# An mLSTM and dilated-attention trunk: whole operands for the 128-column products of layer B, and another order of issue in layer A and at the turn

## The chip, the cores and the metric

The kernel runs on one core of a Trainium2 chip. A core has TensorE for matmuls (PE in the profile; PEld is its weight load), VectorE (DVE), ScalarE (ACT), GpSimd (POOL) and SyncE (SP), which here issues all DMAs. They work in parallel, each in its own order of instructions, and wait for each other through semaphores. The metric is the time of one execution on the device, in microseconds; the median of several runs counts.

## The reference

A sequence of 1024 tokens with 1024 channels goes through two layers. Layer A is an mLSTM: an input projection to three times 2048 channels, a causal convolution, block-diagonal queries, keys and values, a recurrence over chunks with 4 heads, a gate, an output projection and a LayerNorm. Layer B is attention with 8 heads of 128 channels in three groups g = 0, 1, 2, of dilation 1, 4 and 16, which are merged by their softmax denominators.

```python
def mlstm_layer(x, w_in, conv_w, conv_b, wq, wk, wv, w_if, b_if, gn_g, skip, w_out):
    xm, z, o_pre = jnp.split(x @ w_in, 3, axis=-1)
    xc = jax.nn.silu(causal_dwconv(xm, conv_w, conv_b))
    q = headwise(xc, wq)
    k = headwise(xc, wk)
    v = headwise(xm, wv)
...
    h = ((h - mu) * lax.rsqrt(var + LN_EPS)).reshape(bsz, s, INNER_A) * gn_g
    y = (h.astype(x.dtype) + skip * xc) * jax.nn.silu(z)
    return y @ w_out
...
        x = layer_norm(ALPHA * x + y, ln_g[layer], ln_b[layer])
```

In layer B a block of 128 queries sees its own block of 128 keys and, where there is one, the block ahead of it with the same residue of the dilation.

## The kernel before

All products are of 32-bit numbers. `mm3` (lines 97 to 99) makes one of three matmuls in the faster fp32r format: of two operands, each split into a high and a low part, it adds high by high, high by low and low by high. `split` makes the parts: ScalarE copies the high one (line 92), VectorE subtracts it to get the low one (line 93). Where neither operand has been split, a plain F32 matmul of the whole operands is used, as for all of g = 2 (lines 1200 and 1266; each stands in a loop that passes it 8 times in each of the 8 heads, 64 times in all). The larger projections go by Strassen's scheme, in `strassen_steps` and `strassen_wide`, seven block products with sums on VectorE.

The tile framework orders each engine's instructions with a scheduler of its own; the program gives the work, in an order of code, and fixed slots of SBUF (s0 to s52) and banks of PSUM (b0 to b7). `issue_after` binds what it encloses to stand behind a given instruction on its engine. All DMAs are issued by SP, in its one order.

By the time in the profile: up to 379 us the input projection of layer A, its streams of two 128-channel blocks (`stream`) and the z gates. Beside the first streams, `setup` makes on GpSimd the block-diagonal matrices for the values, the gates' weights, and the matrices "A" by which queries and keys meet in the scores (`through`, `spread`, four splits on GpSimd, stores into DRAM). From 391 to 535 us comes the o projection (`strassen_wide`, two pairs of blocks), with the gates' tables between. Attention of layer A (`layer_a_attend`, up to 810 us) goes over 4 heads and 2 halves of the tokens; `prep_q` makes queries, `scores` the first blocks' scores, `finish` joins skip path and gate; the convolved channels xc are loaded before it begins. The out projection (`layer_a_out`, 810 to 987 us) goes over two halves of the tokens; in the second half the first half's rows are transposed to be operands of layer B (`x1`), and `scale_row` applies the LayerNorm's gain and shift for the residual. The last rows are transposed by line 987 at the turn (987 to 1045 us).

Layer B goes over two quads of heads, in each over g = 0, 1, 2, in each over 4 heads: `queries_keys`, `scores`, `attend`. In `attend`, `transposed` turns the weights of up to four 128x128 blocks and splits them, and `av` multiplies them by the values.

Of the kernel before, what the change touches and what calls it, by code (L numbers as in the profile page):

```python
# [11 lines left out]
F32R = mybir.dt.float32r  # L12
# [48 lines left out]
class Kernel:  # L61
# [226 lines left out]
    def strassen_wide(self, raw, x, banks, dest, done, eng):  # L288
# [49 lines left out]
        product(d, b11, x["s1"], True)  # L338
        result(1, 1, u3, d)
        product(c, b21, x["22"], False)  # L340
        result(1, 0, u2, c)
        product(d, b22, x["s4"], False)
        result(0, 1, u2, d)

# [20 lines left out]
    def build(self):  # L365
        nc, tc = self.nc, self.tc
        with ExitStack() as top:
# [35 lines left out]
            self.layer_b()  # L403


    def setup(self):
# [5 lines left out]
        w3 = self.slot(50, (P, 4, NC_A, 4))  # L412
# [3 lines left out]
        wkr = self.slot(52, (P, NC_A, 4, 4))  # L416
        nc.sync.dma_start(wkr, a["wkr"])

        def spread(dst, src, n):
            G.tensor_tensor(dst.rearrange("p c (n j) -> p c n j", j=4),  # L420
                            src.unsqueeze(2).to_broadcast([P, n, 32, 4]),
                            self.mask.unsqueeze(1).unsqueeze(3).to_broadcast([P, n, 32, 4]), op=ALU.mult)

        def through(dst, w, rep, m):

            G.tensor_tensor(rep, rep, w.unsqueeze(3).to_broadcast([P, NC_A, 4, m]), op=ALU.mult)
            G.tensor_tensor(rep[:, :, 0:2], rep[:, :, 0:2], rep[:, :, 2:4], op=ALU.add)
            G.tensor_tensor(dst, rep[:, :, 0], rep[:, :, 1], op=ALU.add)

        self.wv = []  # L430
        for i, c0 in enumerate((0, 7, 14)):
# [4 lines left out]
            spread(t[:, :, 0:P], wvT[:, c0:c0 + n], n)  # L436
        g3 = self.t(cp, [P, 3, NC_A, 8], tag="k2")
        gates = []
        for i, w in enumerate((wqT, wkT, wvT)):
# [3 lines left out]
            through(g, w, rep, 8)  # L443
# [6 lines left out]
        at = w3[:, 3]  # L450
        through(at, wqT, wkr, 4)
        for i in range(2):
            bd = self.slot(51, (P, 8, P))
            spread(bd, at[:, 8 * i:8 * i + 8], 8)
# [7 lines left out]
    def layer_a_project(self):  # L462
# [1112 lines left out]
```

## Time and profile before

| | |
|---|---|
| median of 3 runs | 2061.74 us (2061.1 to 2061.84) |
| the profiled execution, its own time | 2060.43 us |
| its span | 2058.5 us |
| TensorE busy | 1992.0 us, 97% |
| VectorE busy | 1468.4 us, 71% |
| ScalarE busy | 1001.4 us, 49% |
| GpSimd busy | 155.1 us, 8% |
| mean granted clock of TensorE | 0.991 |

The span runs from the first to the last instruction of the profiled execution; its own time is 1.9 us longer. The shares of busy time are means over the span. The granted clock is in parts of full speed.

### The profile page before, as it was taken

What the parts mean: (1) busy time and instruction counts of PE and PEld (TensorE: products, weight loads), DVE (VectorE), ACT (ScalarE), POOL (GpSimd) and SP (SyncE); (2) the same over time, 40 slices, a digit from 0 to 9 for tenths busy, and PEclk for the clock granted to TensorE, in tenths of its full rate; (3) what the DMA queues carried; (4) which work ended last, traced back from release to release, by engine and by line L of the source; (5) the groups of instructions that cost most, each with busy time, mean ns of one, the idle gap of its engine ahead of it and who ended that gap; (6) DMA issues with size and microseconds to landing.
All of it is one profiled execution on the core that took longest, in us unless ns stands there. A gap on an engine that the chain in (4) does not pass through costs nothing.

```text
span 2058.5 us, 28088 instructions
## 1 busy us (share of the span) xinstructions
PE 1992.0 (97%) x10336; PEld 1684.8 (82%) x10336; DVE 1468.4 (71%) x2843; ACT 1001.4 (49%) x1920; POOL 155.1 (8%) x127
## 2 busy tenths in 40 slices
PE   8989999999999999989899999999999999999897
PEld 6868888788788888868788998888888898888786
DVE  8777788674566776475777757756878757757888
ACT  5455555535545543333534636645625635656531
POOL 0130000001145442000000000000000000000000
PEclk9999999999999999999999999999999999999999
DMA  4454565455754443424123131222542232123753
GB/s 166 145 193 168 190 209 180 145 176 201 246 189 171 176 176 135 155 96 160 57 87 123 43 133 52 75 99 103 186 159 101 73 114 72 52 97 110 262 202 123
DMA packets 112945, 288.12 MB, mean 140 GB/s; under 512 B 13028, under 2 KB 34980, under 8 KB 112808
## 3 DMA queue, kind: packets, MB, share of 16 engines
q1 hardware_dynamic: 112808, 286.34, 39.3%
q8 instruction: 81, 1.33, 0.3%
q14 instruction: 56, 0.46, 0.1%
HBM read 200.00 MB, written 86.30 MB: 139 GB/s over the span
## 4 chain that ended last, share of the span: by engine, by line
PE 80%; DVE 9%; DMA 6%; issue 2%; ACT 2%; SPq 0%; DVEq 0%; ACTq 0%
PE b L98 25%; PE b L99 25%; PE b L97 25%; DMA s<-df 3%; DVE s L93 3%; PE b L578 1%; PE b L1223 1%; DVE s L141 1%; PE b L584 1%; PE b L852 1%; DVE s L1340 1%; ACT s L92 1%; DVE s L543 1%; DMA s<-in_w_xm 0%; DMA s<-dc 0%
## 5 line engine op out<-in xcount | busy, mean ns | idle before, releaser
L98 PE MATMUL b<-s,s 128*128 128x512 f32 (+3 forms) x3032 | 1102.1, 366 | 12.1 <-DVE s L93 12.0
L97 PE MATMUL b<-s,s 128*128 128x512 f32 (+2 forms) x3032 | 1082.6, 367 | 26.5 <-ACT s L92 18.3
L99 PE MATMUL b<-s,s 128*128 128x512 f32 (+3 forms) x3032 | 1086.9, 365 | 4.0 <-DVE s L93 3.9
L92 ACT CAST s<-s 128x512 fp32r<-128x512 f32 (+4 forms) x674 | 434.5, 659 | 550.4 <-PE b L99 316.1
L93 DVE TENSOR_TENSOR s<-s,s 128x512 fp32r<-128x512 f32 (+2 forms) x670 | 510.8, 772 | 243.2 <-ACT s L92 240.9
L97 PEld LDWEIGHTS b<-s,s 128*128 128x128 f32 x3032 | 573.6, 190 | 123.2 <-ACT s L92 23.0
L98 PEld LDWEIGHTS b<-s,s 128*128 128x128 f32 x3032 | 576.0, 190 | 100.1 <-DVE s L93 14.3
L99 PEld LDWEIGHTS b<-s,s 128*128 128x128 f32 x3032 | 574.1, 190 | 96.4 <-DVE s L93 7.6
L230 DVE TENSOR_TENSOR s<-s,b 128x512 f32<-128x512 f32 x168 | 114.2, 682 | 56.0 <-PE b L99 52.8
L1210 ACT ACTIVATE s<-s,nmax 128x128 f32<-128x128 f32 (+1 forms) x192 | 84.5, 441 | 38.8 <-DVE nmax L1208 38.0
L224 DVE TENSOR_TENSOR s<-s,b 128x512 f32<-128x512 f32 x112 | 75.8, 680 | 25.2 <-PE b L99 24.8
L93 DVE TENSOR_TENSOR s<-b,s 128x512 fp32r<-128x512 f32 (+1 forms) x96 | 59.0, 630 | 45.7 <-ACT s L92 45.3
L543 DVE SCALAR_TENSOR_TENSOR s<-s,c_convw,s 128x512 f32<-128x512 f32 (+3 forms) x96 | 73.4, 772 | 2.3 <-ACT s L540 1.8
L745 POOL TENSOR_TENSOR s<-s 128x512 fp32r<-128x512 f32 x32 | 43.0, 1357 | 405.9 <-ACT s L744 396.0
L1206 DVE CUSTOM_DVE_ANT_0 s<-b,k 128x128 f32<-128x128 f32 (+1 forms) x192 | 57.8, 346 | 17.5 <-PE b L99 17.4
L786 ACT ACTIVATE s<-s,k 128x128 f32<-128x128 f32 x144 | 47.2, 392 | 41.8 <-DVE s L93 21.5
L243 DVE TENSOR_TENSOR s<-s,s 128x512 f32<-128x512 f32 (+1 forms) x52 | 38.2, 735 | 38.5 <-DMA s<-in_w_xm 15.3
L92 ACT CAST s<-b 128x512 fp32r<-128x512 f32 (+1 forms) x96 | 50.2, 545 | 30.6 <-PE b L99 18.4
L1159 ACT ACTIVATE s<-s 128x512 fp32r<-128x512 f32 x48 | 42.0, 881 | 11.3 <-DVE s L230 11.1
L856 POOL TENSOR_TENSOR s<-s,s 128x512 f32<-128x512 f32 x32 | 42.3, 1337 | 65.5 <-DVE s L855 50.9
L1160 DVE SCALAR_TENSOR_TENSOR s<-s,s 128x512 fp32r<-128x512 f32 x48 | 42.2, 885 | 5.7 <-ACT s L1159 5.3
L1223 PE MATMUL b<-c_ident,s 128*128 128x128 f32 x280 | 44.8, 276 | 0.3 <-ACT s L1210 0.3
(177 smaller groups left out, 1420.6 us busy)
## 6 DMA issues: line engine op xcount, KB each, us to landing
s<-in_w_qk SPq DMA_DIRECT2D x48, 512.0 KB
s<-in_w_out SPq DMA_DIRECT2D x40, 512.0 KB
dp<-s SPq DMA_DIRECT2D x32, 512.0 KB
s<-dp SPq DMA_DIRECT2D x32, 512.0 KB
s<-in_w_z SPq DMA_DIRECT2D x24, 512.0 KB
s<-in_w_v SPq DMA_DIRECT2D x24, 512.0 KB
dg<-s SPq DMA_DIRECT2D x24, 512.0 KB
s<-dg SPq DMA_DIRECT2D x24, 512.0 KB
```

What stands on the lines that cost most here:

```text
L92: self.nc.scalar.copy(h, src)
L93: (l_eng or self.nc.vector).tensor_tensor(l, src, f(h), op=ALU.subtract)
L97: mm(ps, lh, rh, start=start, stop=False, skip_group_check=skip)
L98: mm(ps, lh, rl, start=False, stop=False, skip_group_check=skip)
L99: mm(ps, ll, rh, start=False, stop=stop, skip_group_check=skip)
L224: V.tensor_tensor(o, p, q, op=add)
L230: V.tensor_tensor(o, p[lane][rows], q[lane][rows], op=add)
L543: V.scalar_tensor_tensor(u[i][:, lo:o + 512], xm[i][:, lo - s:o + 512 - s], convw[:, c, 3 - s:4 - s], u[i][:, lo:o + 512], op0=ALU.mult, o ...
L786: A.activation(E[:, i * P:i * P + P], src[:, i * P:i * P + P], AF.Exp, bias=self.bias[:, hd, ig, j:j + 1])
L1206: V.tensor_tensor_reduce(out=dst, in0=sc, in1=bias, op0=ALU.add, op1=ALU.max, scale=1.0, scalar=-3e38, accum_out=mx[:, b:b + 1])
L1210: A.activation(res[b][0], res[b][0], AF.Exp, bias=nm[:, b:b + 1], accum_out=stat[:, 1, g, b:b + 1])
L1223: T.transpose(pt[:, i * P:i * P + P], src, self.ident)
```

## The change

1. Whole operands. In layer B the products of 128 columns are made of whole F32 operands by one matmul instead of three: in each head the four scores of g = 1 that have no block ahead, three value products of g = 0 and four of g = 1. ScalarE writes the whole queries and keys of the first half of g = 1 into slot 52 (`whole`), and copies the turned weights of these products (`pw`); the parts of a split that nobody reads any more are left out.
2. The matrices "A" are no longer made in `setup` but in `setup_scores`, at the first step of the second pair of the o projection.
3. `strassen_wide`, the gates' tables and the attention become generators, so that parts of the latter two can stand between steps of the o projection: attention's preparation behind step 5 of the second pair, first queries and scores behind step 6. xc is loaded head by head. Banks 0 to 3 and 4 to 7 change places in layer A's projection, and two of the z gates stand behind other streams.
4. In the second half of the out projection the splits of `x1` and the residual's scaling are dealt out over steps c = 5 to 10, each bound to stand behind that step's last split.
5. The last transposes of layer A stand behind layer B's first product step.
6. Slots: the residual's scaling keeps slot 52, which the whole operands now use too; some other slots change places.

The core of the diff:

```diff
     def split(self, h, l, src, l_eng=None):
         self.nc.scalar.copy(h, src)
-        (l_eng or self.nc.vector).tensor_tensor(l, src, f(h), op=ALU.subtract)
+        self.last_split = (l_eng or self.nc.vector).tensor_tensor(l, src, f(h), op=ALU.subtract)
...
         product(a, b11, x["11"], True)
+        yield
         for o, p in zip(u2, a):
             A.copy(o, p)
         product(a, b21, x["12"], False)
+        yield
         done(0, 0, a)
...
+            self.attend = self.layer_a_attend()
             self.layer_a_project()
-            self.layer_a_attend()
+            for _ in self.attend:
+                pass
             self.layer_a_out()
...
+    def setup_scores(self):
+        nc, a = self.nc, self.a
+        t = self.slot(40)
+        w, wkr, at = [t[:, lo:hi] for lo, hi in ((0, 64), (64, 320), (320, 384))]
+        w, at = [v.rearrange("p (c i) -> p c i", i=4) for v in (w, at)]
+        wkr = wkr.rearrange("p (c i m) -> p c i m", i=4, m=4)
+        nc.sync.dma_start(w, a["wqT"])
+        nc.sync.dma_start(wkr, a["wkr"])
+        self.through(at, w, wkr, 4)
         for i in range(2):
-            bd = self.slot(51, (P, 8, P))
-            spread(bd, at[:, 8 * i:8 * i + 8], 8)
+            bd = self.slot(41 + i, (P, 8, P))
+            self.spread(bd, at[:, 8 * i:8 * i + 8], 8)
             for j in range(2):
                 cs = slice(512 * j, 512 * j + 512)
-                h, l = self.pair(52)
-                self.split(h, l, bd.rearrange("p c m -> p (c m)")[:, cs], G)
-                nc.sync.dma_start(self.dram["A", i][:, 0, cs], f(h))
-                nc.sync.dma_start(self.dram["A", i][:, 1, cs], f(l))
+                hl = self.slot(43 + j, (P, 2, 512), F32R)
+                self.split(hl[:, 0], hl[:, 1], bd.rearrange("p c m -> p (c m)")[:, cs], nc.gpsimd)
+                nc.sync.dma_start(self.dram["A", i][:, :, cs], f(hl))
...
             mid = last_values(c2)
-            if c2 in (1, 3, 5, 7):
+            if c2 in (0, 2, 5, 7):
                 if c2 == 7:
                     self.w_raw = Ring(32, 33)
-                for _ in gates(z, ones, szs, mid):
+                for _ in gates(z, ones, szs, mid if c2 else None):
                     pass
-                mid, z = None, z + 1
+                mid, z = None if c2 else mid, z + 1
...
-            self.strassen_wide([raw[n] for n in range(4)], x, ((0, 1, 2, 3), (4, 5, 6, 7)), place, sigmoid, V)
-            if pair == 0:
-                columns()
-        self.xc = []
-        for c in range(NC_A):
-            self.xc.append(self.slot((20, 21, 22, 23, 24, 25, 26, 27, 16, 17, 18, 19, 28, 29, 30, 31)[c]))
-            nc.sync.dma_start(self.xc[c], self.dram["xc", c])
+            steps = self.strassen_wide([raw[n] for n in range(4)], x, ((4, 5, 6, 7), (0, 1, 2, 3)), place, sigmoid, V)
+            beside = ({3: lambda: next(tables), 7: lambda: next(tables, None)},
+                      {1: self.setup_scores, 5: lambda: next(self.attend), 6: lambda: next(self.attend)})[pair]
+            for n, _ in enumerate(steps, 1):
+                beside.get(n, lambda: None)()
...
-        q_slots = (44, 45, 46, 47)
+        q_slots = (44, 45, 46, 52)
...
         prep_x(0, 0)
-        prep_q(0, 0)
         prep_v(0, 0)
         st = begin(0, 0)
-        ahead = [scores(0, 0, 0, st), scores(0, 0, 1, st)]
+        yield
+        prep_q(0, 0)
+        ahead = [scores(0, 0, 0, st)]
+        yield
+        ahead.append(scores(0, 0, 1, st))
+        self.xc = []
...
+                if j == 1 and half == 0:
+                    for c in range(HC * hd, HC * hd + HC):
+                        t = self.slot((20, 21, 22, 23, 24, 25, 26, 27, 16, 17, 18, 19, 28, 29, 30, 31)[c])
+                        nc.sync.dma_start(t, self.dram["xc", c])
+                        self.xc.append(t)
...
-                        self.x1["11"], self.x1["12"]
                         gain, shift = self.ln_params(0, 12, 39)
-                        for tb in range(4):
-                            self.scale_row(rows[tb], gain, shift)
-                            nc.sync.dma_start(self.dram["x1", tb], rows[tb])
+                if half and c in (5, 6):
+                    with self.tc.issue_after(self.last_split.ins):
+                        self.x1[("11", "12")[c - 5]]
+                if half and 7 <= c < 11:
+                    with self.tc.issue_after(self.last_split.ins):
+                        self.scale_row(rows[c - 7], gain, shift)
+                    nc.sync.dma_start(self.dram["x1", c - 7], rows[c - 7])
...
-        transposes((4, 5, 6), Ring(0, 1, 2, 3))
-        self.a_last = lambda: transposes((7,), Ring(4, 5))
+        self.a_last = lambda: [transposes((4, 5, 6), Ring(2, 3, 4, 5)), transposes((7,), Ring(6, 7))]
...
-                next(steps), next(steps)
+                next(steps)
+                self.a_last()
+                next(steps)
                 self.w_raw, u_slots, self.u_slots = Ring(50, 51), self.u_slots, Ring(13)
-                ahead = gates(0, (52, 48), ((7,), (1,), (2,), (3,)))
+                ahead = gates(0, (47, 48), ((7,), (1,), (2,), (3,)))
                 next(ahead), next(ahead)
                 self.u_slots = u_slots
-                self.a_last()
...
+            whole = self.slot(52, (P, 2, 4, P)) if g == 1 else None
...
+                if g == 1 and half == 0:
+                    A.activation(whole[:, i], sv, AF.Copy, scale=scale)
+                    if i == 0:
+                        return
...
+                    elif g == 1 and b % 2 == 0:
+                        T.matmul(ps[:, o:o + w], whole[:, 0, b // 2], whole[:, 1, b // 2], start=True, stop=True,
+                                 skip_group_check=True)
...
-                    self.split(ph[:, 0:n], pl[:, 0:n], pt[:, 0:n])
+                    m = n - P * n_whole
+                    self.split(ph[:, 0:m], pl[:, 0:m], pt[:, 0:m])
+                    if n_whole:
+                        pw = self.t(cp, [P, 2, P], tag="pw", bufs=2)
+                        A.copy(pw[:, 0:n_whole].rearrange("p j n -> p (j n)"), pt[:, m:n])
+                        return ph, pl, pw
...
+            def av_whole(bank, o, kb, p2, j, start):
+                T.matmul(po[bank][:, o:o + P], v[kb][2], p2[2][:, j], start=start, stop=True,
+                         skip_group_check=True)
...
                     if b2 == 1:
-                        av(0, 384, P, 3, p2, 256, False)
-                        av(1, 0, P, 3, p2, 384, True)
+                        av_whole(0, 384, 3, p2, 0, False)
+                        av_whole(1, 0, 3, p2, 1, True)
                     elif b2 == 3:
-                        av(1, 384, P, 7, p2, 256, False)
+                        av_whole(1, 384, 7, p2, 0, False)
                     else:
-                        av(bank, (b % 4) * P + P, 256, b + 1, p2, 256, False)
+                        av(bank, (b % 4) * P + P, b + 1, p2, 256, False)
...
-                    p2 = transposed(q0, q1[:, 0:P], q1[:, P:256])
+                    p2 = transposed(q0, q1[:, 0:P], q1[:, P:256], n_whole=1)
                     at = 256 * (r % 2)
-                    av(r // 2, at, 256, 2 * r, p2, 0, r % 2 == 0)
-                    av(r // 2, at + P, P, 2 * r + 1, p2, 256, False)
+                    av(r // 2, at, 2 * r, p2, 0, r % 2 == 0)
+                    av_whole(r // 2, at + P, 2 * r + 1, p2, 0, False)
```

On ScalarE at the start of attention: before, with L854 the skip scaling of xc, L636 the o gate's activation, and the casts from banks (b) the high parts of the first queries.

```order
L854 ACTIVATE s_739_4314<-s_739_4314,c_skip_3147 128x512 x2
L854 ACTIVATE s_740_4316<-s_740_4316,c_skip_3147 128x512 x2
L636 ACTIVATE s_725_4278<-s_725_4278 128x512 x2
L636 ACTIVATE s_726_4279<-s_726_4279 128x512 x2
L92 CAST s_749_4336<-b_748_4332 128x512
L92 CAST s_751_4343<-b_750_4339 128x512
L854 ACTIVATE s_741_4318<-s_741_4318,c_skip_3147 128x512 x2
L92 CAST s_753_4350<-b_752_4346 128x512
L854 ACTIVATE s_742_4320<-s_742_4320,c_skip_3147 128x512 x2
L92 CAST s_755_4357<-b_754_4353 128x512
```

After, where L870 is the skip scaling and L653 the o gate:

```order
L92 CAST s_733_4249<-b_732_4245 128x512
L92 CAST s_735_4256<-b_734_4252 128x512
L870 ACTIVATE s_1144_6468<-s_1144_6468,c_skip_3118 128x512 x2
L870 ACTIVATE s_1145_6470<-s_1145_6470,c_skip_3118 128x512 x2
L653 ACTIVATE s_747_4356<-s_747_4356 128x512 x2
L92 CAST s_737_4263<-b_736_4259 128x512
L92 CAST s_739_4270<-b_738_4266 128x512
L653 ACTIVATE s_748_4357<-s_748_4357 128x512 x2
```

The first two casts now stand ahead of the skip scaling, the next two behind two pairs of it.

On VectorE in the second half of the out projection: before, with L909 and L910 the residual's gain and shift, L991 an eviction of transposes, and L93 the subtractions, of `x1` from s_1356 to s_1365, of w_out and of the running rows otherwise.

```order
L93 TENSOR_TENSOR s_1373_7853<-s_1359_7783,s_1372_7852 128x1024
L909 TENSOR_TENSOR s_1316_7512<-s_1316_7512,s_1378_7864 128x1024
L909 TENSOR_TENSOR s_1318_7537<-s_1318_7537,s_1378_7864 128x1024
L909 TENSOR_TENSOR s_1320_7562<-s_1320_7562,s_1378_7864 128x1024
L991 TENSOR_SCALAR s_1365_7809<-b_1367_7816,c_lnT_7008 128x512
L909 TENSOR_TENSOR s_1327_7611<-s_1327_7611,s_1378_7864 128x1024
L93 TENSOR_TENSOR s_1375_7857<-s_1362_7796,s_1374_7856 128x1024
L910 TENSOR_TENSOR s_1316_7512<-s_1316_7512,s_1379_7865 128x1024
L910 TENSOR_TENSOR s_1318_7537<-s_1318_7537,s_1379_7865 128x1024
L910 TENSOR_TENSOR s_1320_7562<-s_1320_7562,s_1379_7865 128x1024
L93 TENSOR_TENSOR s_1377_7861<-s_1365_7809,s_1376_7860 128x1024
L910 TENSOR_TENSOR s_1327_7611<-s_1327_7611,s_1379_7865 128x1024
```

After, where L934 and L935 are gain and shift:

```order
L93 TENSOR_TENSOR s_1381_7916<-s_1356_7767,s_1380_7915 128x1024
L93 TENSOR_TENSOR s_1383_7920<-s_1359_7780,s_1382_7919 128x1024
L93 TENSOR_TENSOR s_1384_7923<-s_888_5094,s_1384_7923 128x512
L93 TENSOR_TENSOR s_1392_7964<-s_889_5096,s_1392_7964 128x512
L93 TENSOR_TENSOR s_1387_7929<-s_1385_7926,s_1386_7928 128x1024
L93 TENSOR_TENSOR s_1389_7957<-s_1362_7793,s_1388_7956 128x1024
L93 TENSOR_TENSOR s_1391_7961<-s_1365_7806,s_1390_7960 128x1024
L93 TENSOR_TENSOR s_1396_8000<-s_1015_5779,s_1396_8000 128x512
L93 TENSOR_TENSOR s_1395_7970<-s_1393_7967,s_1394_7969 128x1024
L934 TENSOR_TENSOR s_1316_7509<-s_1316_7509,s_1370_7845 128x1024
L93 TENSOR_TENSOR s_1399_8006<-s_1397_8003,s_1398_8005 128x1024
L934 TENSOR_TENSOR s_1318_7534<-s_1318_7534,s_1370_7845 128x1024
```

Subtractions of the running products now stand between those of `x1`, and the scaling comes behind them, an operation at a time.

On TensorE at the turn: before, the last products of the out projection and then the transposes (L987), of which 26 stand in a row.

```order
L98 MATMUL b_1369_7823<-s_1427_8177,s_1424_8171 128x512
L99 MATMUL b_1369_7823<-s_1426_8176,s_1424_8171 128x512
L987 MATMUL b_1447_8353<-c_ident_246,s_1428_8180 128x128
L987 MATMUL b_1447_8353<-c_ident_246,s_1430_8211 128x128
L987 MATMUL b_1448_8358<-c_ident_246,s_1428_8180 128x128
L987 MATMUL b_1448_8358<-c_ident_246,s_1430_8211 128x128
```

After, with the transposes as L1012 and layer B's first products in banks b_1456 and b_1457, 48 of which stand ahead of the first transpose:

```order
L99 MATMUL b_1457_8366<-s_1488_8499,s_1389_7957 128x256
L97 MATMUL b_1457_8366<-s_1488_8499,s_1388_7956 128x256
L1012 MATMUL b_1475_8452<-c_ident_246,s_1428_8177 128x128
L1012 MATMUL b_1475_8452<-c_ident_246,s_1430_8208 128x128
L1012 MATMUL b_1475_8452<-c_ident_246,s_1432_8239 128x128
L98 MATMUL b_1457_8366<-s_1488_8499,s_1388_7956 128x256
L99 MATMUL b_1457_8366<-s_1488_8499,s_1389_7957 128x256
L1012 MATMUL b_1476_8457<-c_ident_246,s_1428_8177 128x128
L1012 MATMUL b_1476_8457<-c_ident_246,s_1430_8208 128x128
L1012 MATMUL b_1476_8457<-c_ident_246,s_1432_8239 128x128
```

The transposes have moved behind and in between products of layer B.

## Rows read from the trace of the kernel before

**Rows 1.** The page: the span, and section 1

```profile
span 2058.5 us, 28088 instructions
...
PE 1992.0 (97%) x10336; PEld 1684.8 (82%) x10336; DVE 1468.4 (71%) x2843; ACT 1001.4 (49%) x1920; POOL 155.1 (8%) x127
```

**Rows 2.** TensorE's waits over the span: us, times, longest

```profile
PE b L97 <- ACT s L92: 18.3, 11, 6.4
PE b L98 <- DVE s L93: 12.0, 5, 4.8
```

**Rows 3.** Stretches: length, busy time (instructions) of PE, PEld, DVE, ACT, POOL, clock, DMA share, GB/s

```profile
120.00:140.00 20.00, 14.68 (x63) 10.98 (x62) 18.27 (x28) 10.57 (x20) 7.60 (x4) 0.91 0.67 249
480.00:520.00 40.00, 40.00 (x178) 33.12 (x177) 20.03 (x30) 28.34 (x52) 1.50 (x1) 1.00 0.69 245
535.00:550.00 15.00, 10.78 (x46) 7.71 (x45) 5.29 (x8) 9.26 (x16) 0.00 (x0) 1.00 0.86 303
900.00:930.00 30.00, 22.24 (x99) 16.66 (x98) 21.16 (x22) 13.37 (x18) 0.00 (x0) 0.89 0.45 163
985.00:1000.00 15.00, 10.88 (x67) 9.15 (x66) 8.91 (x31) 8.74 (x12) 0.00 (x0) 0.89 0.35 141
1010.00:1040.00 30.00, 26.52 (x182) 24.45 (x181) 26.85 (x33) 15.72 (x22) 0.00 (x0) 0.94 0.08 28
1079.00:1088.00 9.00, 7.25 (x24) 5.22 (x23) 6.95 (x11) 2.89 (x5) 0.00 (x0) 0.81 0.41 152
1550.00:1800.00 250.00, 250.00 (x1478) 221.06 (x1478) 181.76 (x388) 129.50 (x282) 0.00 (x0) 1.00 0.24 83
```

**Rows 4.** Line 1266, and timelines of TensorE: start, us, instruction

```profile
L1266 PE MATMUL b<-s,s x128: 270/275/275, 1417.3 to 1968.0; 128*128 128x128 f32 x128
...
1417.30 1.05 PE L1266 MATMUL b<-s,s 128*128 128x128 f32 x8
...
552.04 0.27 PE L97 MATMUL b<-s,s 128*128 128x128 f32 x1
552.15 0.27 PE L98 MATMUL b<-s,s 128*128 128x128 f32 x1
```

**Rows 5.** Groups of two shapes: busy us, mean ns, idle before

```profile
L1159 ACT ACTIVATE s<-s 128x512 fp32r<-128x512 f32 x48 | 42.0, 881 | 11.3 <-DVE s L230 11.1
...
L93 POOL TENSOR_TENSOR s<-s,s 128x512 fp32r<-128x512 f32 x4 | 6.7, 1663 | 16.0 <-ACT s L92 16.0
```

**Rows 6.** Timeline beside the first streams

```profile
118.96 0.68 DVE L93 TENSOR_TENSOR s<-s,s 128x512 fp32r<-128x512 f32 x1
...
124.66 2.24 POOL L420 TENSOR_TENSOR s<-s,em 128x1024 f32<-128x1024 f32 x1
125.06 2.39 DVE L93 TENSOR_TENSOR s<-s,s 128x512 fp32r<-128x512 f32 x1
...
129.47 0.41 PE L584 MATMUL b<-s,k 128*16 128x512 f32 x1 [4.45 <-ACT s L92]
```

**Rows 7.** Timeline at the start of attention

```profile
535.77 2.63 ACT L854 ACTIVATE s<-s,c_skip 128x512 f32<-128x512 f32 x4 [4.78 <-DMA s<-dc]
...
541.00 0.68 PE L97 MATMUL b<-s,s 128*128 128x512 f32 x2 [2.34 <-ACT s L92]
```

**Rows 8.** Timelines of VectorE and TensorE in the out projection

```profile
907.66 3.49 DVE L909 TENSOR_TENSOR s<-s,s 128x1024 f32<-128x1024 f32 x3
...
921.60 0.80 PE L98 MATMUL b<-s,s 128*128 128x512 f32 x1 [4.81 <-DVE s L93]
```

**Rows 9.** Timeline at the turn to layer B

```profile
990.65 4.38 PE L987 MATMUL b<-c_ident,s 128*128 128x128 f32 x21 [3.38 <-ACT s L972]
```

**Rows 10.** Timeline at the first heads of layer B

```profile
1074.39 0.32 SPq L1053 DMA_DIRECT2D s<-dx  x1
...
1078.03 1.22 DVE L909 TENSOR_TENSOR s<-s,s 128x1024 f32<-128x1024 f32 x1 [1.73 <-DMA s<-dx]
...
1080.48 0.19 PEld L97 LDWEIGHTS b<-s,s 128*128 128x128 f32 x1 [1.13 <-ACT s L92]
```

More of the change, by code (lines that the diff above doesn't have):

```diff
@@ L411, in setup @@
         self.mask = self.const("mask32", [P, 32], tag="em")
-        w3 = self.slot(50, (P, 4, NC_A, 4))
+        w3 = self.slot(50, (P, 3, NC_A, 4))
         for i, n in enumerate("qkv"):
@@ L415, in setup @@
         wqT, wkT, wvT = w3[:, 0], w3[:, 1], w3[:, 2]
[L416 to L428, printed above, removed]
         self.wv = []
@@ L435, in setup @@
                 self.wv.append(t[:, c])
-            spread(t[:, :, 0:P], wvT[:, c0:c0 + n], n)
+            self.spread(t[:, :, 0:P], wvT[:, c0:c0 + n], n)
         g3 = self.t(cp, [P, 3, NC_A, 8], tag="k2")
@@ L442, in setup @@
             g = g3[:, i]
-            through(g, w, rep, 8)
+            self.through(g, w, rep, 8)
             gates.append(g)
@@ L503, in layer_a_project @@
         halves = lambda h: slice(512 * h, 512 * h + 512)
-        ones = ((0,), (1,), (2,), (3,))
+        ones = ((4,), (5,), (6,), (7,))
         def gates(c2, banks, szs, mid=None, raw=None):
@@ L520, in layer_a_project @@
         quarters = lambda p: [t[:, 512 * i:512 * i + 512] for t in wz[p] for i in range(2)]
-        for _ in zip_longest(*[gates(p, ((p,), (p,), (4 + p,), (p,)), szs, raw=quarters(p)) for p in range(4)]):
+        for _ in zip_longest(*[gates(p, ((4 + p,), (4 + p,), (p,), (4 + p,)), szs, raw=quarters(p)) for p in range(4)]):
             pass
@@ L609, in layer_a_project @@
             A.copy(gs[:, 512 * half:512 * half + 512], psg[half][0:16, :])
-        columns = self.gate_tables(gs, gx, pv)
+        tables = self.gate_tables(gs, gx, pv)
+        next(tables)
         self.w_hl, self.u_slots = Ring(36, 37, 49, 47), Ring(8, 9, 10, 11)
@@ L705, in gate_tables @@
                           self.dram["G"].unsqueeze(0).to_broadcast([P, HA, 64]))
-        def columns():
-            cols = self.bank(pv)[:, 0:64].rearrange("p (s b h) -> p s b h", s=2, h=4)
-            for s, r in enumerate((ar, em)):
-                for j in range(8):
-                    T.transpose(cols[:, s, j], r[:, j * P:j * P + P], self.ident[0:4, 0:4])
-            self.em = self.t(cp, [P, 8, HA], tag="em")
-            V.tensor_copy(self.em, cols[:, 1])
-            for h in range(HA):
-                V.tensor_tensor(self.bias[:, h], cols[:, 0, :, h].unsqueeze(1).to_broadcast([P, 8, 8]), self.bias[:, h],
-                                op=ALU.add)
-        return columns
+        yield
+        cols = self.bank(pv)[:, 0:64].rearrange("p (s b h) -> p s b h", s=2, h=4)
+        for s, r in enumerate((ar, em)):
+            for j in range(8):
+                T.transpose(cols[:, s, j], r[:, j * P:j * P + P], self.ident[0:4, 0:4])
+        self.em = self.t(cp, [P, 8, HA], tag="em")
+        V.tensor_copy(self.em, cols[:, 1])
+        for h in range(HA):
+            V.tensor_tensor(self.bias[:, h], cols[:, 0, :, h].unsqueeze(1).to_broadcast([P, 8, 8]), self.bias[:, h],
+                            op=ALU.add)
     def layer_a_attend(self):
@@ L1143, in head_values @@
             at = lambda b: (b // 4, b % 4) if g == 0 else (b % 2, b // 2)
-            return [(h[:, at(b)[0], at(b)[1]], l[:, at(b)[0], at(b)[1]]) for b in range(8)]
+            whole = lambda half, t: v[half][i].rearrange("p (t n) -> p t n", t=4)[:, t, cs]
+            return [(h[:, at(b)[0], at(b)[1]], l[:, at(b)[0], at(b)[1]], whole(*at(b))) for b in range(8)]
         def queries_keys(h, g):
@@ L1163, in queries_keys @@
             self.strassen(self.quarters(a["w_qk"][g, h]), x, ones, None, done, V)
-            return [(None, th[i], tl[i]) for i in range(2)]
+            return [(whole, th[i], tl[i]) for i in range(2)]
         def table(h, g):
@@ L1175, in scores @@
         def scores(h, g, qk, stat):
-            (_, qh, ql), (_, kh, kl) = qk
+            (whole, qh, ql), (_, kh, kl) = qk
             tb = table(h, g)
```

41 lines of the change are left out of this document (27 added, 14 removed).

## The prediction

> **What bounds the kernel now.** I read the page first. TensorE is busy for 97% of the span [rows 1]: the most that better order can return is the 66 us in which it is idle, and what it loses while its granted clock is low. VectorE at 71% and ScalarE at 49% are not the bound over the whole, but each can be over a few microseconds. The waits of TensorE, sorted by releaser, come second: the largest are for the two halves of a split, the copy on ScalarE (18.3 us in 11 waits) and the subtraction on VectorE (12.0 us in 5) [rows 2]. Eleven and five: a few places lose, not a steady rate. So the third view is a table of stretches, where each loss can be priced. The reader is to see in it that the long stretch of attention in layer B is full (250.00 of 250 us, clock 1.00), and that five short stretches in layer A, in the turn to layer B and at its first heads are not [rows 3]. I price a stretch by its length less TensorE's busy time, plus its length times what the granted clock lacks of 1 (a mean of the two levels, 2.4 and 1.2 GHz). That gives 5.3 + 1.8 = 7.1 us (120 to 140), 4.2 (535 to 550), 7.8 + 3.3 = 11.1 (900 to 930), 4.1 + 1.7 = 5.8 (985 to 1000), 3.5 + 1.8 = 5.3 (1010 to 1040) and 1.7 + 1.7 = 3.5 (1079 to 1088), 37 us in all. The change can gain in two ways: fewer passes where TensorE is full, and fewer of these holes. The second is bounded by 37 us.
>
> **Whole operands.** In each of the 8 heads, 11 products of 128 columns (4 scores of g = 1, 3 value products of g = 0, 4 of g = 1) go from three passes to one F32 matmul, 88 in all. They lie where TensorE is full, so each pass saved counts. A 128-column pass starts 0.11 us behind the one ahead of it [rows 4], so a triple costs 0.33. F32 matmuls of that shape stand in the trace: line 1266 is reached 64 times in the code and has 128 records, two to a product, and eight records take 1.05 us from first start to last end; with 0.275 for one, the spacing is (1.05 - 0.275) / 7 = 0.11 [rows 4]. A whole product thus costs 0.22, and saves 0.11: 88 x 0.11 = **-9.8 us**. The Trainium skill (FP8 and Floating Point Precision, TensorE Precision Notes) speaks against this: true FP32 takes four passes through the array, which at the row's spacing would be 0.44 a product, and the sum below would end at 2050 instead of 2030. The row counts two. I take the row, and four records at 0.11, +9.8, as the other bound: the operands here come from other slots and copies, and the trace has no scores product of this kind.
>
> The copies that feed them are ScalarE's. Per head two more 128x512 copies of queries and keys less the one that is dropped, 0.88 us each [rows 5], and six short copies out of PSUM against shorter splits: some 2 us more in a head. VectorE loses one 128x512 operation and half of some subtractions. In the full stretch ScalarE is busy for 129.5 of 250 us [rows 3], about half; 16 us over 8 heads lie under TensorE, at no cost as long as no score waits for its copy. If one did in every head, it would be the 0.9 us of the copy, 7 us in all; I keep that in the costs below.
>
> **Weights of the attention, moved out of the start.** Beside the first streams GpSimd spreads and splits them. While its 2.24 us spread runs, a VectorE subtraction takes 2.39 us where its neighbour took 0.68, and TensorE then idles 4.45 us behind ScalarE [rows 6]. Two spreads (4.5 us), four splits (6.7) [rows 5, 6] and the products ahead of them leave this place; the spreads for the values stay, and some streams still fall beside them. The price was 7.1; I take **-5**, bounds 0 and -7.1. The same 11 us and more of GpSimd now run beside the second o pair. If they stretch VectorE there as here, each of the six costs up to 1.7 us of VectorE (2.39 - 0.68), 10 us; VectorE is busy 20.03 of 40 us in 480 to 520 [rows 3], so TensorE should be covered, and I charge part of it below.
>
> **Attention begun inside the o projection.** Now TensorE idles 2.34 us at 541 for a query split; ScalarE stood in front of them with the skip scaling, held 4.78 us by a load of xc [rows 7]. In the changed order the first two query casts stand ahead of the skip scaling, and the first scores lie among the last o products, so this wait and the lesser ones behind it should go: **-3.5** of 4.2, bounds 0 and -4.2. The xc loads now come in at each head's second block. The old ones were loaded by the end of the projection; they are late only if ScalarE's scaling blocks later casts, since it stands directly behind two of them.
>
> **Out projection, second half.** VectorE does eight 128x1024 operations of the residual's gain and shift in a block (3.49 us for three, so 9.3 for all) with the x operands' splits between them, and TensorE waits 4.81 us behind the splits that follow [rows 8]. The new order puts the splits of the running products first and deals the rest out over four steps, queued behind each step's last split. VectorE has the time: it is busy 21.16 of 30 us there [rows 3]. **-9** of 11.1; the near bound is the 4.8 wait less something given back, -4, the far one -10.3, since the transposes' own waits stay.
>
> **Turn to layer B.** TensorE runs the transposes right behind the last out product, so it waits 3.38 us for ScalarE's normalisation, and then starts and stops at the pace of their evictions [rows 9]. In the changed kernel 48 products of 256 columns of layer B's first step stand there; at no less than the 0.11 us of a 128-column pass they cover at least 5.3 us, and the transposes are dealt in among later ones. Two stretches, 5.8 + 5.3 = 11.1. But VectorE is busy 26.85 of the 30 us in 1010 to 1040 [rows 3]: the x operands that it makes are needed as early as before, and come out of the same transposes, now a little later. So I take only the first stretch and a little: **-6**, bounds +2 and -11.1.
>
> **Residual and w_qk.** At 1074 the residual's load is issued ahead of the w_qk loads and VectorE scales beside them; TensorE waits 0.71 us for a copy, and over 1079 to 1088 the clock is 0.81 [rows 3, 10]. The slot that the residual shares is now taken by the whole queries and keys, so it moves behind g = 1's scores: **-2.5** of 3.5, bounds 0 and -3.5.
>
> **New costs.** GpSimd beside the o projection, the copies, and waits for the one slot that `whole` and the residual share: **+4**, bounds 0 and +10 + 7 + 4 (a microsecond for the slot in each of 4 heads) = +21, which need all the covers above to fail.
>
> **Sum.** -9.8 - 5 - 3.5 - 9 - 6 - 2.5 + 4 = -31.8. The profiled execution took 2060.43 us, so 2028.6; the median is 1.3 above it: **2030**.
>
> **Rivals.**
> 1. *The holes move* (0.18). Layer A's order is one chain of splits on two engines; a split brought forward pushes another back, above all at the turn, where VectorE is full for 30 us. For it: that row. Against it: VectorE's idle time in the stretches just ahead. Half of the 26 us of order terms comes back: 2030 + 13 = 2043.
> 2. *Four passes* (0.04): 2050, worked out above.
> 3. *Attention isn't really earlier* (0.10). Only queries and first scores can gain: the casts of the values stand ahead of the skip scaling in the old order too; and a split of queries still needs a bank that the o products give back. Then the 3.5 stay: 2033.
> 4. *Slower: the single slot* (0.08). In quad 0's g = 1 heads the residual load waits for the scores' last reader of the slot, then come load, two scalings (2.4 us) and store, before the next head's `whole` may be written; on the queue the next w_qk loads stand behind that load. The cost of such a round is about 8 us: 3.6 from the load's issue at 1074.39 to the first scaling at 1078.03 [rows 10], 2.4, and a store of some 2. If w_qk came so late that a head lost all 8 and the clock with it (the 9 us stretch at 1079 lost 3.5, half in clock), four heads lose 4 x (8 + 2) = 40: 2030 + 40 = 2070. It decides above 8 a head (32 / 4); a head that loses 7 to 9 leaves the time as it was. Against it: the load has a whole head to land.
>
> **How the numbers follow.** The forecast has 0.60 and by itself 2020 to 2040. A measurement of this kernel tells 0.2%, 4 us, from no change. Everything but rival 4 is faster; of its 0.08 I give 0.05 to slower and 0.03 to the same: 0.92, 0.03, 0.05. For the range: the far bounds of all terms give -46, so 2016; above, rival 1 with 4 us on it, 2047. Left out are rivals 2 and 4 (0.12) and the tails.
>
> **What would show it.** The records of the triple of 128 columns fall by 88 each; the new whole products have two records each, 0.11 apart. The wait of the gates' product at 129 is gone, and the subtraction beside it takes 0.7. No wait of over 1 us at the start of attention. Between 900 and 930 TensorE is idle under 3 us at clock 1.00. Behind the out projection comes no 3.4 us wait. I am wrong if TensorE's idle time stays near 66 us with other names in the list, if the whole products have four records, or if in quad 0's g = 1 heads TensorE waits for a product whose weights were issued behind the residual.

## The result, and the profile after

The changed kernel took 2031.45 us (median of 4, 2027.09 to 2035.07) where the kernel before took 2061.42 on the same chip: 30.0 us less, a ratio of 0.9854 (0.9832 to 0.9877). The forecast was 2030, and 31.8 us less than the profiled execution. The profiled execution after took 2033.71 us.

The page after, the lines that answer to [rows 1]:

```profile
span 2031.9 us, 28005 instructions
PE 1978.9 (97%) x10248; PEld 1674.3 (82%) x10248; DVE 1455.0 (72%) x2835; ACT 1010.9 (50%) x1976; POOL 153.3 (8%) x127
```

TensorE is busy 13.1 us less, in 88 records less (at 0.11 us each these are 9.7), and idle for 53.0 us instead of 66.5. So the gain has two halves: less work, and smaller holes. The share of 97% says neither; it is the same in both.

The stretches after, in the columns of [rows 3], each set to where the same part of the program runs now:

```profile
120.00:140.00 20.00, 19.12 (x90) 15.16 (x90) 15.48 (x28) 10.65 (x20) 0.00 (x0) 1.00 0.65 238
535.00:550.00 15.00, 14.63 (x79) 12.65 (x78) 10.21 (x22) 8.85 (x18) 0.00 (x0) 1.00 0.86 293
890.00:920.00 30.00, 28.09 (x135) 22.45 (x134) 20.17 (x22) 19.16 (x26) 0.00 (x0) 1.00 0.25 89
980.00:1000.00 20.00, 16.60 (x99) 14.29 (x97) 19.24 (x22) 15.93 (x26) 0.00 (x0) 0.91 0.08 27
1000.00:1020.00 20.00, 16.05 (x119) 15.84 (x120) 15.83 (x21) 5.39 (x8) 0.00 (x0) 0.91 0.04 14
1055.00:1075.00 20.00, 20.00 (x100) 16.93 (x99) 14.29 (x30) 8.49 (x19) 0.00 (x0) 1.00 0.16 54
```

Priced as in the prediction: 0.9 us beside the first streams (7.1 before), 0.4 at the start of attention (4.2), 1.9 in the out projection (11.1), none at the first heads (3.5). But the two stretches at the turn cost 3.4 + 1.8 and 3.95 + 1.8, 11 us, as much as the two before.

The waits of TensorE from 975 to 1020 us (total, times, longest), after:

```profile
PE b L98 <- DVE s L93: 3.7, 1, 3.7
PE b L97 <- ACT s L92: 2.8, 2, 2.3
```

And the groups of TensorE's products of 128 columns after (L1238 scores, L1286 values):

```profile
L1286 PE MATMUL b<-pw,s 128*128 128x128 f32 x112 | 20.3, 274 | 0.0
L1238 PE MATMUL b<-s 128*128 128x128 f32 x64 | 12.0, 273 | 0.0
L99 PE MATMUL b<-s,s 128*128 128x128 f32 x40 | 11.0, 275 | 0.0
```

176 records for 88 products: two each. 40 records of each pass of a triple are left.

### The profile page after: what moved, and what is told of

It reads as the page before. It is cut to its first block, busy times and chain, and to the rows that moved or that the text cites. A ratio compares the mean times of both kernels' runs of the same rounds, so it can differ in the third digit from the quotient of the medians.

```text
span 2031.9 us, 28005 instructions
## 1 busy us (share of the span) xinstructions
PE 1978.9 (97%) x10248; PEld 1674.3 (82%) x10248; DVE 1455.0 (72%) x2835; ACT 1010.9 (50%) x1976; POOL 153.3 (8%) x127
## 4 chain that ended last, share of the span: by engine, by line
PE 76%; DVE 10%; DMA 9%; ACT 2%; issue 2%; SPq 0%; POOL 0%; DVEq 0%; ACTq 0%
PE b L97 23%; PE b L99 23%; PE b L98 23%; DMA s<-df 3%; DVE s L93 3%; PE b L593 1%; PE b L1263 1%; ACT s L92 1%; DMA s<-in_w_out 1%; DVE s L141 1%; PE b L599 1%; PE b L868 1%; DVE s L1391 1%; DMA s<-in_w_o 1%; PE b L1286 1%
## 5 line engine op out<-in xcount | busy, mean ns | idle before, releaser
L97 PE MATMUL b<-s,s 128*128 128x512 f32 (+2 forms) x2944 | 1067.4, 371 | 23.1 <-ACT s L92 18.0
L98 PE MATMUL b<-s,s 128*128 128x512 f32 (+2 forms) x2944 | 1079.8, 368 | 9.1 <-DVE s L93 9.1
L99 PE MATMUL b<-s,s 128*128 128x512 f32 (+2 forms) x2944 | 1064.8, 368 | 4.5 <-DVE s L93 4.2
L93 DVE TENSOR_TENSOR s<-s,s 128x512 fp32r<-128x512 f32 (+2 forms) x670 | 507.7, 769 | 248.0 <-ACT s L92 245.8
L97 PEld LDWEIGHTS b<-s,s 128*128 128x128 f32 x2944 | 558.1, 190 | 119.4 <-ACT s L92 23.8
L98 PEld LDWEIGHTS b<-s,s 128*128 128x128 f32 x2944 | 559.5, 190 | 96.8 <-DVE s L93 10.7
L99 PEld LDWEIGHTS b<-s,s 128*128 128x128 f32 x2944 | 557.1, 190 | 95.1 <-DVE s L93 7.9
L93 DVE TENSOR_TENSOR s<-b,s 128x512 fp32r<-128x512 f32 (+1 forms) x96 | 51.0, 551 | 37.6 <-ACT s L92 37.3
L92 ACT CAST s<-b 128x512 fp32r<-128x512 f32 (+1 forms) x96 | 43.2, 478 | 24.8 <-PE b L99 13.7
L1391 DVE TENSOR_TENSOR s<-s,s 128x1024 f32<-128x1024 f32 x21 | 25.7, 1223 | 30.1 <-DMA s<-df 30.0
```

What stands on the lines that cost most here:

```text
L93: self.last_split = (l_eng or self.nc.vector).tensor_tensor(l, src, f(h), op=ALU.subtract)
L97: mm(ps, lh, rh, start=start, stop=False, skip_group_check=skip)
L98: mm(ps, lh, rl, start=False, stop=False, skip_group_check=skip)
L99: mm(ps, ll, rh, start=False, stop=stop, skip_group_check=skip)
L1391: V.tensor_tensor(o, o, fb, op=ALU.mult)
```

## The experiments

Each time stands beside the kernel before, measured with it on the same chip. Single runs of one kernel are up to 12 us apart, so differences of 3 us between kernels are at the edge of what these runs tell, and the traces decide.

Much of this scatter comes late. The first merge of layer B begins with transposes of `stat` (in `factors`; L1281 before, L1332 after). From there to the end, eleven of the traces, of the changed kernel and of runs 1 and 3 to 11, have the same instructions in the same order on TensorE, VectorE and ScalarE, and yet this part takes from 637.8 to 644.6 us. What a change does ahead of it is better read from when that first merge starts, in the kernel before and in the changed one (number, ns, first and last start):

```profile
L1281 PE MATMUL b<-c_ident,stat x8: 270/270/272, 1414.4 to 1955.5; 128*48 128x128 f32 x8
```

```profile
L1332 PE MATMUL b<-c_ident,stat x8: 270/270/272, 1387.4 to 1925.7; 128*48 128x128 f32 x8
```

That is 27.0 us earlier, about as much as the two spans differ (26.6); in run 5, the changed kernel once more, it starts at 1386.2.

**1. The whole operands alone**, in the kernel before.

```diff
+            whole = self.slot(52, (P, 2, 4, P)) if g == 1 else None
...
-                        self.mm3(ps[:, o:o + w], qh[:, bs], ql[:, bs], kh[:, ks], kl[:, ks], True, True, skip=True)
+                        T.matmul(ps[:, o:o + w], whole[:, 0, b // 2], whole[:, 1, b // 2], start=True, stop=True,
+                                 skip_group_check=True)
...
-                    av(r // 2, at + P, P, 2 * r + 1, p2, 256, False)
+                    av_whole(r // 2, at + P, 2 * r + 1, p2, 0, False)
```

and the rest of part 1 of the change; the mm3 shown stays for the other scores.

> The kernel before with the whole operands alone; all of its order in layer A and at the turn stays. The slot that whole operands and residual share comes with them, so the residual moves too. Theory: 88 products at two records each save 0.11 us, -9.8, and the residual's move -2.5: about 2049 us, 12 below the kernel before; whole products with two records each in the trace. Rival, four records to a product: +9.8 - 2.5, about 2069. Rival, the copies on ScalarE or the single slot take it back: 2057 or more, with TensorE waiting in g = 1 of the first quad.

2050.44 us against 2061.06 (0.996, 0.9948 to 0.9973): 10.6 less by the medians, 8.2 by the ratio, the residual's move included. In its trace the new lines again have 64 and 112 records, and the hole of [rows 10] is gone:

```profile
1070.00:1095.00 25.00, 25.00 (x117) 20.92 (x117) 17.41 (x34) 10.23 (x22) 0.00 (x0) 1.00 0.18 64
```

Four records are out; the price of two holds, though part of it is the residual's.

**2. The order alone.**

```diff
-                    av_whole(r // 2, at + P, 2 * r + 1, p2, 0, False)
+                    av(r // 2, at + P, P, 2 * r + 1, p2, 256, False)
```

and so on through part 1, which is undone in the changed kernel.

> The changed kernel with the products of 128 columns as three passes again; all of the new order stays, and the residual is free again to come ahead of the w_qk loads. Theory: 9.8 + 2.5 above the changed kernel's 2031.5, so about 2044, with the wait behind the residual back (0.7 us and a lower clock at the first heads). Rival, the gain was all order and the whole products are worth nothing: 2031 to 2034. Rival, they cost four passes: about 2022.

2037.15 us (0.9892, 0.9873 to 0.9911), 23.9 less than before by the medians, some 6 more than the changed kernel (8 by the ratios). Here the residual's loads do come ahead of the w_qk loads again:

```profile
1052.36 0.32 SPq L1081 DMA_DIRECT2D s<-dx  x1
1052.82 2.38 SPq L177 DMA_DIRECT2D s<-in_w_qk  x2
```

This is SyncE's queue in this kernel: start, length, line. Over 1050 to 1070 its TensorE is idle 0.74 us, at full clock:

```profile
1050.00:1070.00 20.00, 19.26 (x85) 15.36 (x84) 17.27 (x25) 6.88 (x12) 0.00 (x0) 1.00 0.46 175
```

That is the 0.71 us wait for a copy that the prediction names, back again. Another stands some 20 us ahead of it, behind VectorE, whose first scaling of the residual (L934) comes in there:

```profile
1033.74 1.23 DVE L934 TENSOR_TENSOR s<-s,s 128x1024 f32<-128x1024 f32 x1 [0.80 <-DMA s<-in_ln_g]
```

```profile
1036.31 0.47 PE L97 MATMUL b<-s,s 128*128 128x512 f32 x1 [1.38 <-DVE s L224]
...
1059.03 0.50 PE L97 MATMUL b<-s,s 128*128 128x512 f32 x1 [0.71 <-ACT s L92]
```

From 1020 to 1075 us TensorE idles 2.1 us in this kernel and not at all in the changed one, which scales the residual later. So the residual's place matters in the new order too; only the fall of the clock doesn't come back.

**3. The matrices A in `setup` again.**

```diff
-                      {1: self.setup_scores, 5: lambda: next(self.attend), 6: lambda: next(self.attend)})[pair]
+                      {5: lambda: next(self.attend), 6: lambda: next(self.attend)})[pair]
```

with `setup` as it stood before.

> The changed kernel with the matrices A made in setup again, beside the first streams. Theory: the hole at 120 to 140 us returns, +5 to +7, so 2036.5 to 2038.5, with the wait of the gates' product for ScalarE (4.5 us) back. Rival, GpSimd beside the o projection had taken back what the hole gave: within 2 us of 2031.5.

2035.23 us (0.988, 0.9861 to 0.9899), some 4 more than the changed kernel, and the first merge starts at 1393.4, 6 to 7 us later. The hole is back, first the stretch and then the wait in this kernel's trace (L593 is here the gates' product):

```profile
120.00:140.00 20.00, 14.89 (x62) 11.03 (x61) 17.43 (x26) 11.04 (x22) 7.61 (x4) 0.83 0.68 249
```

```profile
PE b L593 <- ACT s L92: 4.4, 1, 4.4
```

In the changed kernel GpSimd does this work between 410 and 466 us. The dearest subtraction of VectorE beside it:

```profile
421.24 1.94 POOL L417 TENSOR_TENSOR s<-s,em 128x1024 f32<-128x1024 f32 x1 [2.92 <-ACT s L711]
...
430.21 1.29 POOL L93 TENSOR_TENSOR s<-s,s 128x512 fp32r<-128x512 f32 x1 [4.41 <-ACT s L92]
```

```profile
430.69 1.37 DVE L93 TENSOR_TENSOR s<-s,s 128x512 fp32r<-128x512 f32 x1 [2.79 <-ACT s L92]
```

It takes 1.37 us instead of 0.68, and TensorE isn't idle there; between 400 and 500 us it idles 0.52 us in all, where before it idled none.

**4. x1 splits and scaling in one piece again.**

```diff
+                        self.x1["11"], self.x1["12"]
                         gain, shift = self.ln_params(0, 12, 39)
...
-                if half and c in (5, 6):
-                    with self.tc.issue_after(self.last_split.ins):
-                        self.x1[("11", "12")[c - 5]]
...
+                        for tb in range(4):
+                            self.scale_row(rows[tb], gain, shift)
+                            nc.sync.dma_start(self.dram["x1", tb], rows[tb])
```

> The changed kernel with the x1 splits and the residual's scaling in one piece again, right behind the first blocks of the second half. Theory: the hole of the out projection returns, +9 (4.8 us wait for a subtraction, lesser ones and the clock), so about 2040.5. Rival, the hole had only moved to the turn: about 2036 or less, with fewer waits at the turn to layer B.

2040.83 us (0.9906, 0.9888 to 0.9924), some 9 to 10 more; the first merge starts at 1394.5, 7 to 8 us later. The same stretch and the same wait are back:

```profile
890.00:920.00 30.00, 22.64 (x95) 17.14 (x96) 22.83 (x24) 14.52 (x19) 0.00 (x0) 0.89 0.52 193
```

```profile
PE b L98 <- DVE s L93: 4.9, 1, 4.9
```

At the turn TensorE waits 6.2 us from 960 to 1020 us, instead of 7.4; at most a microsecond of the gain had been borrowed from there.

**5. The changed kernel once more**, as a reference for 6 to 8; 1 to 4 and 9 to 12 are set to its first runs.

> The changed kernel once more, unaltered, on the chip of the three runs beside it, as their reference. Expected: 29 to 31 us below the kernel before, as at first (30).

2031.86 us against 2062.12 (0.9848, 0.9831 to 0.9864), 30.3 less.

**6. The transposes ahead of layer B's first step again.**

```diff
-        self.a_last = lambda: [transposes((4, 5, 6), Ring(2, 3, 4, 5)), transposes((7,), Ring(6, 7))]
+        transposes((4, 5, 6), Ring(0, 1, 2, 3))
+        self.a_last = lambda: transposes((7,), Ring(4, 5))
```

and the call of `a_last` at its old place.

> The changed kernel with layer A's last transposes ahead of layer B's first product step again. Theory of the prediction: the transposes' waits return, +6 over the changed kernel. Rival, which the trace of the changed kernel speaks for: there TensorE is idle for 3.4 and 3.9 us in two stretches of 20 us at the turn, with the clock at 0.91 in both, 11 us in all as before the change; VectorE's subtractions for the x operands set the pace, so undoing the move costs nothing, within 2 us.

2031.83 us (0.9862, 0.9843 to 0.9882): by the medians no difference, by the ratios 2.9 us more, and the first merge starts at 1388.9, 1.5 to 2.7 us later. The wait for the LayerNorm is back at the place of [rows 9], while the 3.7 us wait for VectorE has become several of less than 2; the waits of TensorE from 960 to 1020 us in this kernel:

```profile
PE b L1012 <- ACT s L997: 3.4, 1, 3.4
PE b L98 <- DVE s L93: 2.2, 2, 1.8
PE b L99 <- DVE s L93: 2.2, 2, 1.4
PE b L97 <- ACT s L237: 0.5, 1, 0.5
```

They are 8.3 us in all; the changed kernel has 7.4 there (3.7, 2.8, 0.6 and 0.3). So the move is worth little, between nothing and 3 us.

**7. The attention begun behind the o projection again**, with all loads of xc there.

```diff
-                      {1: self.setup_scores, 5: lambda: next(self.attend), 6: lambda: next(self.attend)})[pair]
+                      {1: self.setup_scores})[pair]
```

> The changed kernel with the attention begun behind the whole o projection again, and all loads of xc there. Theory: +3.5 to +5 over the changed kernel; the waits for query splits (2.3 and 1.6 us) return at the start of attention. Rival: the scheduler had the preparation early enough anyway: within 1.5 us, with no such wait.

2035.08 us (0.987, 0.9851 to 0.9888), some 3 more than 5; the first merge starts at 1391.6, 4 to 5 us later. A wait for a query split stands at 536:

```profile
536.26 0.91 PE L97 MATMUL b<-s,s 128*128 128x512 f32 x3 [3.08 <-ACT s L92]
```

**8 and 9. The z gates behind streams 1, 3, 5 and 7 again**, twice.

```diff
-            if c2 in (0, 2, 5, 7):
+            if c2 in (1, 3, 5, 7):
...
```

> The changed kernel with the z gates behind streams 1, 3, 5 and 7 again. In the changed kernel's trace TensorE idles 1.9 us between 80 and 100 us at a clock of 0.91, with VectorE waiting for a z weight. Theory: this early place costs 2 to 4 us, and undoing it gains them, -2 to -4. Rival: without it the first streams come closer together and VectorE, full there, opens holes between 100 and 140 us: +1 to +4.

> The changed kernel with the z gates behind streams 1, 3, 5 and 7 once more, as it came out 6 us faster, though its trace shows no gain before 1400 us, where the order of instructions is the same. If the place of the gates is the cause: again 4 to 8 us below the changed kernel, so 2024 to 2028 where the kernel before takes 2061. If it was the spread of single runs: within 3 us of 2031.5.

2025.41 us against 2062.12 (0.9824, 0.9808 to 0.984), and then 2028.64 against 2059.93 (0.9851, 0.9835 to 0.9868). The first is 6 us faster than the changed kernel beside it, the second has nearly its ratio (0.9851 against 0.9848). In both traces the instructions behind 400 us stand in the same order as in the changed kernel, and the first merge starts at 1386.1 and 1385.3 us, within 2.1 us of the changed kernel's two traces. The rest of what they gain lies behind, where this part takes 637.8 us in both: that is the low end of the scatter, not the place of the gates. Why the four runs of 8 lie nearly all below those of 5 stays open; a gain of more than a microsecond or two is not shown.

**10. One x operand of the turn on GpSimd**, as 6 speaks for VectorE as the bound there.

```diff
-                                       "s4": (28, 29, 30, 31)}, {})
+                                       "s4": (28, 29, 30, 31)}, {"s4": nc.gpsimd}, s4_eng=nc.gpsimd)
```

> The changed kernel with the sums and the subtractions of one x operand, s4, on GpSimd instead of VectorE (four operations of 128x1024, 1.22 us each on VectorE). GpSimd is idle at the turn. Theory: there VectorE is busy without a gap from 982 to 1008 us and sets the pace, so the wait of 3.7 us at 1004 shrinks or goes, and the time falls by 2 to 5 us. Rival: something else sets it (the transposes' evictions or the LayerNorm), and nothing changes, within 1.5 us. Rival: GpSimd holds VectorE up as it did beside the first streams: +2 to +6, with subtractions of 128x1024 on VectorE of over 1.5 us.

2037.73 us against 2059.93 (0.9895, 0.9877 to 0.9913), slower by 6 than the changed kernel. The second rival had the sign, but the way is longer than it said. GpSimd in this kernel, and ScalarE:

```profile
990.90 10.11 POOL L141 TENSOR_TENSOR s<-s,s 128x1024 f32<-128x1024 f32 x1 [175.96 <-DVE s L141]
```

```profile
1001.04 3.03 ACT L92 CAST s<-s 128x1024 fp32r<-128x1024 f32 x4 [6.72 <-POOL s L141]
```

```profile
1005.12 0.80 PE L97 MATMUL b<-s,s 128*128 128x256 f32 x2 [4.89 <-ACT s L92]
```

ScalarE comes to the cast of s4 early, waits 6.72 us for GpSimd's sum, and the casts of the running weights are queued behind; TensorE waits for these. VectorE is held up too, in its subtractions from 1002 to 1013 us (number, us, mean ns), which take 0.68 and 1.22 elsewhere:

```profile
L93 DVE TENSOR_TENSOR s<-s,s 128x512 fp32r<-128x512 f32 x4 | 6.1, 1554 | 3.9 <-ACT s L92 3.9
L93 DVE TENSOR_TENSOR s<-s,s 128x1024 fp32r<-128x1024 f32 x2 | 4.6, 2294 | 0.0
```

So this run says nothing on the bound.

**11. Both 8 and 10**, as a candidate for a faster kernel.

> Both together, the z gates as before and s4 on GpSimd, as a candidate for a kernel faster than both. If the two gains add: 2020 to 2024. If neither is one: about 2031.

2035.3 us (0.9881, 0.9866 to 0.9896); it is 10's loss again.

**12. The x operand s4 left out.** Layer B uses s2 in its place.

```diff
         def make(n):
+            if n in alias:
+                return x[alias[n]]
             if n[0] == "s":
...
-                                       "s4": (28, 29, 30, 31)}, {})
+                                       "s4": (28, 29, 30, 31)}, {}, alias={"s4": "s2"})
```

> The changed kernel without the x operand s4 at the turn to layer B: its two sums and two splits are left out, and s2 is used in its place, so layer B computes other numbers with the same instructions of TensorE. VectorE has four operations of 128x1024 less there (4.6 us), ScalarE two casts, and GpSimd stays idle. Theory: VectorE sets the pace at the turn, so the wait for its subtraction at 1004 us (3.7) shrinks to under 1 us and layer B begins 3 to 6 us earlier. Rival: the transposes or ScalarE set it; then a wait of about the same length stands there and layer B begins less than 1 us earlier.

2023.36 us against 2060.37 (0.9824, 0.9797 to 0.9851), 37.0 less than before and some 7 less than the changed kernel; the first merge starts at 1382.1, 4 to 5 us earlier. The waits of TensorE from 975 to 1020 us are those for ScalarE and the transposes; the one for VectorE is gone:

```profile
PE b L97 <- ACT s L92: 2.8, 2, 2.3
PE b L1014 <- ACT s L1020: 0.6, 1, 0.6
PE b L1014 <- ACT s L1116: 0.3, 1, 0.3
```

and the second stretch of the turn is nearly full:

```profile
980.00:1000.00 20.00, 16.76 (x91) 14.29 (x90) 19.28 (x22) 14.04 (x23) 0.00 (x0) 0.83 0.08 27
1000.00:1020.00 20.00, 19.59 (x163) 19.59 (x164) 13.84 (x20) 5.66 (x9) 0.00 (x0) 1.00 0.04 14
```

So VectorE sets the pace in the second stretch. ScalarE's two casts of s4 left with VectorE's operations, but TensorE's waits for ScalarE's casts are 2.8 us in both kernels; these stay in the first stretch.

## Why the prediction was right, term by term

The time and the sign came out, and 30 us of 31.8. The terms are not all as forecast; what undoing each costs, by the medians, and by when the first merge starts:

| term | forecast | by the medians | to the first merge |
|---|---|---|---|
| whole operands and residual | -9.8 - 2.5 | -10.6 alone, -6 in the new order | -4.8 alone, -3 to -4 in the new order |
| weights moved | -5 | -4 | -6 to -7 |
| attention begun early | -3.5 | -3 | -4 to -5 |
| out projection | -9 | -9 to -10 | -7 to -8 |
| turn to layer B | -6 | 0 | -1.5 to -3 |
| new costs | +4 | | about +1 seen, at the shared slot |

That the sum came so near is luck in part: the turn gave at most half of its term, and what it lacks is made up by costs that were booked at 4 and seen at about 1, and by somewhat more from the weights and the attention.

**Whole operands.** The step from L1266 held: two records, 0.11 us apart. The four passes of the Trainium skill (FP8 and Floating Point Precision, TensorE Precision Notes) don't show as four records, nor as a time of 0.44. The four records of two products, and the three transposes behind them, stand as

```profile
1161.08 0.61 PE L1286 MATMUL b<-pw,s 128*128 128x128 f32 x4
1161.52 0.49 PE L1263 MATMUL b<-c_ident,s 128*128 128x128 f32 x3
```

in the changed kernel, 0.44 us from the one start to the other for two products. ScalarE's copies cost nothing that shows in the full stretch. Half of the 9.8 should come behind the first merge; that part took 644.1 us before and takes 637.8 to 644.6 with whole operands, so single traces don't tell these 4.9 us from the scatter.

**Weights, attention, out projection.** Each of these was a wait with a name in the trace of before, each is gone after, and 3, 7 and 4 bring it back at about its old length (4.4 for 4.45, 3.08 for 2.34, 4.9 for 4.81). The cost that GpSimd's work was to have beside the o projection hardly came: VectorE has the time there.

**The turn** is the step that failed. The prediction took the first of two stretches as won, since 48 products would cover the LayerNorm. They do, and its 3.4 us wait is gone. TensorE's new waits there are 3.7 us for VectorE and 2.8 for ScalarE's casts. The prediction put VectorE's busy 26.85 of 30 us down to the second stretch only. In the changed kernel it fills the first as well (19.24 of the 20 us from 980): its chain begins earlier and runs on nearly without a gap, and TensorE, having its covered products behind it, meets its end waiting. That was the first rival, at this one place, and it took at least half of the term; 12 shows the chain to be the bound of the second stretch. What would shorten the 2.8 us for ScalarE no run tells. Ahead of the first merge no other new hole of 2 us opened.

**Residual.** The mechanism held, and the size about: with the residual moved the hole is gone in the old order (1, 3.5 us) and in the new one, and with the loads at their old place (2) TensorE idles 2.1 us again. The clock, half of the old price, stays at 1.00 there.

**The single slot**, the slower rival, shows in small, and with it one of the three signs of being wrong that the prediction names. In the changed kernel the residual's load goes ahead of the w_qk loads at the first quad's g = 1, and ScalarE waits for these:

```profile
1256.00 0.62 ACT L92 CAST s<-s 128x512 fp32r<-128x512 f32 x1 [3.01 <-DMA s<-in_w_qk]
...
1258.80 0.38 PE L97 MATMUL b<-s,s 128*128 128x256 f32 x1 [0.61 <-ACT s L92]
1259.81 0.50 PE L97 MATMUL b<-s,s 128*128 128x512 f32 x1 [0.63 <-ACT s L1192]
```

TensorE loses 1.2 us, once, far from the 8 per head that would have decided. Run 1, where the slot is shared too, has the same two waits; run 2, where it isn't, has neither.

## What to carry to other kernels

A wait with a name, a length and idle time on the engine ahead of it is worth its length and the clock that falls with it: three such terms came out within a microsecond or so. Where the engine that releases the wait is busy without a gap, as VectorE at the turn, moving the waiting work moved most of the wait; count that engine's operations over the whole stretch before booking a gain. An engine that is idle is no help by that alone: a sum moved to GpSimd took 10 us, and what was queued behind its reader cost more than VectorE had gained.

## What was not expected of the hardware

A sum of 128x1024 on GpSimd took 10.11 us beside VectorE's operations at the turn, by a record that the page calls rough, though ScalarE's wait of 6.72 us for it agrees; the next such sum, in the same run, took 2.81. VectorE's operations beside it kept their length, the last of them, of an unbroken row, being

```profile
997.55 1.22 DVE L141 TENSOR_TENSOR s<-s,s 128x1024 f32<-128x1024 f32 x1
```

GpSimd's sum ended 2.24 us after this one, not far from the 2.81 of the next, and in run 11, where it took 10.11 us too, 2.23 us after. So it looks as if it went ahead only once VectorE had stopped; two runs show this, and none tests it. VectorE's subtractions beside GpSimd's next operations ran at about twice their length (1.55 for 0.68 us, 2.29 for 1.22), as at 430 us in the changed kernel (1.37), and at 3.5 times beside the first streams before [rows 6]. The Trainium skill (SBUF — State Buffer, SBUF: two separate sides) describes an exclusive lock on a port pair that these two engines share. The stretched operations agree with it; no run here parts the lock from another cause.
